# A two-layer mixer trunk on Trainium2: S5's direct products on four quarters of the array, retention's position factors moved to its values, S5's angles doubled in one run, LRU gates in small PSUM banks

## The chip, the core and the metric

The kernel runs on one core of one Trainium2 chip. TensorE multiplies, VectorE (DVE in the profile), ScalarE (ACT) and GpSimd (POOL) work on vectors, SyncE (SP) issues the transfers. The metric is device microseconds of one execution of the whole program; lower is better.

## What is computed

A trunk of two layers (`DEPTH = 2`) over 512 positions of width 1024 in float32. Each layer normalises its input, projects it, runs four token mixers of width 512 in parallel, gates and projects each, sums them under sigmoid gates and adds the projection of the sum:

```python
for l in range(DEPTH):
    u = rmsnorm(h, norm_gain[l])
    proj = u @ w_in[l]
    ...
    o_gla = gla_mix(...) * jax.nn.silu(gg)
    o_ret = retention_mix(rq, rk, rv, ...) * jax.nn.silu(rg)
    o_lru = rglru_mix(lx, ...) * jax.nn.silu(lg)
    y5 = jax.nn.gelu(s5_scan(su, ...))
    ...
    for bi, o in enumerate((o_gla, o_ret, o_lru, o_s5)):
        gate = jax.nn.sigmoid(u @ w_merge_gate[l, bi])
        merged = merged + gate * (o @ w_branch[l, bi])
    h = h + merged @ w_out[l]
return rmsnorm(h, final_norm_gain)
```

In retention, queries and keys are rotated by position, and factors that depend on the position in a chunk of 64 and on the head weight them: keys by `k_w` in the state, queries by `q_w` in front of the state, a decay between the two in the scores; each head's output is then normalised by its own mean and variance. RG-LRU needs per block two gates, sigmoids of a product with the block's convolved input, and a scan along time. S5 is a diagonal state-space model of 32 groups with 64 complex states, in blocks of 128 positions.

## The kernel before

**Products in three passes.** A float32 product is split into a high and a low part. Each weight tile of 128x1024 comes from memory into one of two raw buffers; ScalarE writes its high part (`hi`, L271), VectorE its low part (`lo`, L272), each into one of four buffers; then TensorE multiplies three times (L297 to L299 where the weight is the stationary operand, L391 to L393 in `proj_w` where the activations are). A raw buffer is free for the next transfer when the low part is written. All weights pass in one order of use.

**PSUM.** Three banks (`psm`, in the trace `pm`) serve the large products, five small ones (`pss`, `ps`) the rest. A bank comes back when the engine that evacuates it has read it.

**Order.** TensorE executes in the order in which the program is written. The order on the other engines is set by a scheduler that goes by its own estimates. Background work (attention, S5, LRU) is written as generators, which a tick after every few large matmuls advances by a step.

**The places of the change.** `s5_params` makes, for each layer, tables of sines and cosines by doubling: VectorE doubles an angle (`double`, L461 to L463) and copies the pair to `s5w` (L529, L530), and GpSimd (`grow`, L516 to L521) makes the next level of the table from it. It is written ahead of products that VectorE evacuates with L940 and L941 in the first layer, and ahead of the last merge (L1081) for the second. `s5_scan` has 8 groups per layer: `states` (L627) and `direct` (L637) multiply a group's input, `outputs` (L671) adds the state's part, ScalarE evacuates (L677); then comes a scan on VectorE. In `direct` the rows 64 to 127 of the array go with the columns 64 to 127, and the rows 0 to 63 with the columns 0 to 63. In `lru_block` a convolution (L1010) gives the block's input, split into xh and xl (L306); gate(0) and gate(1) (L1017) multiply it, ScalarE takes them through tanh, exp and square root (L1022 to L1037), VectorE and GpSimd combine them (L1030 to L1038), and VectorE scans (L1039, its result used by L1040). In retention `rotate` takes a tile of queries and keys: L1096 weights by the position factors (`gtab`) as it evacuates, L1103 (GpSimd) and L1105 multiply with sine and cosine, L1109 adds. The projection of the values follows, which ScalarE evacuates (L1121).

## Time and profile before

| what | value |
| --- | --- |
| median of 3 runs | 1243.51 us (1240.65 to 1243.98) |
| the profiled execution | 1242.54 us |
| its span in the trace | 1240.8 us |
| mean granted clock of TensorE, share of full speed | 0.991 |
| TensorE busy | 1205.1 us, 97% |
| VectorE busy | 816.8 us, 66% |
| ScalarE busy | 516.5 us, 42% |
| GpSimd busy | 508.0 us, 41% |
| moved by DMA | 127.89 MB, mean 103 GB/s |

Every time in the text is counted from the start of the span. Matmuls are pipelined, so the rows of two neighbours overlap; the distance of their starts is what one costs. "idle <- X" at a row's end is how long the engine had nothing to do before it, and what ended that.

### The profile page before, as it was taken

To read this page: it belongs to the slowest core of one execution; us is meant where nothing else is said; L and a number is where in the kernel's file an instruction comes from. 1 tells how busy PE (TensorE), PEld (TensorE's weight loads), DVE (VectorE), ACT (ScalarE), POOL (GpSimd) and SP (SyncE) were. 2 spreads that over 40 slices of the span, in tenths; PEclk is the share of its full clock that TensorE was granted. 3 is DMA by queue.
4 is the path that set the end of the run, shared out by engine and by line. 5 is a ranking of instruction groups with operands and counts; after the bars stand their busy time and mean duration, and the time that the engine had idled before them with its cause. 6 is when DMAs were issued, how large, how long until landed. Compare 5 with 4: busy or idle time off the path is not lost.

```text
span 1240.8 us, 17527 instructions
## 1 busy us (share of the span) xinstructions
PE 1205.1 (97%) x6649; PEld 990.5 (80%) x6649; DVE 816.8 (66%) x1479; ACT 516.5 (42%) x798; POOL 508.0 (41%) x547
## 2 busy tenths in 40 slices
PE   9989999989999999999999999999799999999997
PEld 7878768868888787888898887788688888888886
DVE  6686878686688678644355367776957986436433
ACT  5613475333434532432355235644244453324322
POOL 1473328988765159100201013397977551000001
PEclk9999999998999999999999999999899999999999
DMA  6334222322522442433343242233233233433322
GB/s 193 121 91 149 78 79 96 98 68 69 167 80 81 127 136 73 119 102 102 104 137 95 92 151 62 84 96 89 72 106 120 69 120 103 138 99 102 93 77 85
DMA packets 48758, 127.89 MB, mean 103 GB/s; under 512 B 6465, under 2 KB 19105, under 8 KB 48674
## 3 DMA queue, kind: packets, MB, share of 16 engines
q1 hardware_dynamic: 48098, 125.73, 32.6%
q8 instruction: 52, 0.85, 0.3%
q10 hardware_dynamic: 576, 1.05, 0.2%
q14 instruction: 32, 0.26, 0.1%
HBM read 118.37 MB, written 8.39 MB: 102 GB/s over the span
## 4 chain that ended last, share of the span: by engine, by line
PE 79%; DVE 8%; ACT 4%; POOL 4%; issue 2%; DMA 1%; SPq 0%; POOLq 0%; DVEq 0%; ACTq 0%
PE pm L297 20%; PE pm L298 19%; PE pm L299 19%; PE pm L391 4%; PE pm L392 4%; PE pm L393 4%; PE pm L370 3%; DVE lo L272 2%; PE ps L756 1%; PE ps L627 1%; PE ps L671 1%; PE ps L767 1%; PE ps L637 1%; PE ps L778 1%; ACT hi L271 1%
## 5 line engine op out<-in xcount | busy, mean ns | idle before, releaser
L272 DVE TENSOR_TENSOR lo<-raw,hi 128x1024 fp32r<-128x1024 f32 (+1 forms) x196 | 268.4, 1370 | 189.5 <-ACT hi L271 188.6
L297 PE MATMUL pm<-uh,hi 128*128 128x512 f32 x960 | 378.3, 394 | 7.3 <-ACT ac L1027 3.3
L299 PE MATMUL pm<-uh,lo 128*128 128x512 f32 x960 | 374.2, 390 | 0.0
L298 PE MATMUL pm<-ul,hi 128*128 128x512 f32 x960 | 373.9, 389 | 0.0
L271 ACT ACTIVATE hi<-raw 128x1024 fp32r<-128x1024 f32 (+1 forms) x196 | 207.4, 1060 | 399.0 <-PE pm L298 274.9
L297 PEld LDWEIGHTS pm<-uh,hi 128*128 128x128 f32 x960 | 180.2, 188 | 50.7 <-ACT ac L1027 5.0
L299 PEld LDWEIGHTS pm<-uh,lo 128*128 128x128 f32 x960 | 180.2, 188 | 38.1
L298 PEld LDWEIGHTS pm<-ul,hi 128*128 128x128 f32 x960 | 180.3, 188 | 36.3
L1226 POOL TENSOR_TENSOR ac<-c4a,S 128x512 f32<-128x512 f32 x2 | 2.6, 1295 | 248.6 <-DVE c4a L1224 248.6
L297 PE MATMUL pm<-oh,hi 128*128 128x512 f32 x256 | 101.0, 395 | 0.0
L299 PE MATMUL pm<-oh,lo 128*128 128x512 f32 x256 | 99.8, 390 | 0.0
L298 PE MATMUL pm<-ol,hi 128*128 128x512 f32 x256 | 99.7, 389 | 0.0
L391 PE MATMUL pm<-hi,uh 128*128 128x512 f32 x128 | 53.7, 419 | 12.8 <-DVE s L1096 12.8
L316 POOL TENSOR_TENSOR ty<-ty,c 128x4 f32<-128x4 f32 x16 | 17.6, 1103 | 102.9 <-DVE ty L314 102.6
L297 PEld LDWEIGHTS pm<-oh,hi 128*128 128x128 f32 x256 | 48.0, 188 | 11.2 <-issue 1.4
L299 PEld LDWEIGHTS pm<-oh,lo 128*128 128x128 f32 x256 | 48.0, 188 | 10.1
L298 PEld LDWEIGHTS pm<-ol,hi 128*128 128x128 f32 x256 | 48.1, 188 | 9.7
L392 PE MATMUL pm<-hi,ul 128*128 128x512 f32 x128 | 52.0, 406 | 0.0
L393 PE MATMUL pm<-lo,uh 128*128 128x512 f32 x128 | 51.9, 405 | 0.0
L1081 DVE SCALAR_TENSOR_TENSOR s<-s,pm 128x512 f32<-128x512 f32 x48 | 32.7, 682 | 14.8 <-PE pm L299 14.8
L391 PEld LDWEIGHTS pm<-hi,uh 128*128 128x128 f32 x128 | 25.4, 198 | 19.0 <-DVE s L1096 13.6
L647 DVE TENSOR_TENSOR r<-ps,cos 128x256 f32<-128x256 f32 x32 | 13.3, 422 | 39.5 <-ACT sw L646 39.5
(336 smaller groups left out, 2093.0 us busy)
## 6 DMA issues: line engine op xcount, KB each, us to landing
raw<-in_wch SPq DMA_DIRECT2D x192, 512.0 KB, 3.6
raw<-in_wgv SPq DMA_DIRECT2D x4, 544.0 KB, 4.7
uc<-in_x SPq DMA_DIRECT2D x4, 512.0 KB, 5.5
bc<-in_s5bc SPq DMA_DIRECT2D x16, 128.0 KB, 2.1
su_dram<-c4a SPq DMA_DIRECT2D x4, 512.0 KB, 2.8
uc<-su_dram SPq DMA_DIRECT2D x32, 64.0 KB, 2.6
y_dram<-uc SPq DMA_DIRECT2D x4, 512.0 KB, 4.8
v<-y_dram SPq DMA_DIRECT2D x32, 64.0 KB, 2.6
```

The source lines that it names most:

```text
L271: act.activation(hi, raw, AF.Copy)
L272: dve.tensor_tensor(lo, raw, hi.bitcast(F32), SUB)
L297: pe.matmul(ps, lh, rh, start=i == 0, stop=False)
L298: pe.matmul(ps, lh, rl, start=False, stop=False)
L299: pe.matmul(ps, ll, rh, start=False, stop=i == n - 1)
L316: pool.tensor_tensor(r, ms, neghalf[:, :n], ALU.pow)
L370: pe.matmul(ps[:, j], a[:, k, ts], ws[kh][b][:, k % 4], start=k == i == 0, stop=k == KD - 1 and i == 2)
L391: pe.matmul(ps[tt], xh(k, ts), wh, start=k == 0, stop=False)
L392: pe.matmul(ps[tt], xl(k, ts), wh, start=False, stop=False)
L393: pe.matmul(ps[tt], xh(k, ts), wl, start=False, stop=k == KD - 1)
L647: dve.tensor_tensor(r1[:, gg::2], pst[gg], cos[:, gg::2], MUL)
L1081: dve.scalar_tensor_tensor(t, t, 1.0, ps, op0=ADD, op1=MUL)
```

## The change

Four edits in one. `direct` sends each half of the rows to both halves of the columns in turn, so that its four products use all four quarters of the array; `outputs` and the way in which the result is read back follow that layout, and the evacuation becomes four pieces. In retention `gtab` no longer weights queries and keys: ScalarE copies the tile out of PSUM (L1100), VectorE and GpSimd rotate it (L1106, L1111, L1114), the values take the factor as they are evacuated, one piece per head (L1130), and the small constant in the variance is weighted to match. In `s5_params` all doublings are made in one run into a buffer with a place for each level. And `gate` takes a small bank.

```diff
-        wx = one("s5w", [P, 2, G])
+        wx = one("s5w", [P, 7, 2, G])
...
-        c4, sg4 = wx[:, 0], wx[:, 1]
-        double(sn, cs, sg4, c4)
-        double(sg4, c4, sn, cs)
-        dve.tensor_scalar(sg4, sn, sgn[:, 1:2], None, op0=MUL)
-        dve.tensor_copy(c4, cs)
+        double(sn, cs, ps_, pc_)
+        double(ps_, pc_, sn, cs)
+        dve.tensor_scalar(wx[:, 0, 0], sn, sgn[:, 1:2], None, op0=MUL)
+        dve.tensor_copy(wx[:, 0, 1], cs)
+        for i in range(6):
+            double(wx[:, i, 0], wx[:, i, 1], wx[:, i + 1, 0], wx[:, i + 1, 1])
...
-        for tab, nlev in ((bt, 4), (at, 3)):
+        for tab, lev0, nlev in ((bt, 0, 4), (at, 4, 3)):
...
-                grow(tab, 1 << lev, c4, sg4)
-                double(sg4, c4, sn, cs)
-                dve.tensor_copy(sg4, sn)
-                dve.tensor_copy(c4, cs)
+                grow(tab, 1 << lev, wx[:, lev0 + lev, 1], wx[:, lev0 + lev, 0])
...
-                    pe.matmul(st["bank"][gg][r, (2 + pr) * P:(3 + pr) * P], tz[r, pr], u2[r, pr],
-                              start=alone and pr == 0, stop=False, skip_group_check=True)
+                    o = 64 * (gg ^ pr)
+                    pe.matmul(st["bank"][gg][o:o + 64, (2 + pr) * P:(3 + pr) * P], tz[r, pr], u2[r, pr],
+                              start=alone, stop=False, skip_group_check=True)
...
-            for gg in range(2):
-                r = slice(64 * gg, 64 * gg + 64)
-                act.activation(u2[r], bank[gg][r, 2 * P:].rearrange("p (a b) -> p a b", a=2), AF.Copy)
+            for pr in range(2):
+                for half in range(2):
+                    r = slice(64 * half, 64 * half + 64)
+                    act.activation(u2[r, pr], bank[half ^ pr][r, (2 + pr) * P:(3 + pr) * P], AF.Copy)
...
             def gate(i):
-                g = psm()
+                g = pss()
...
-            xg = s2([P, 2, HEADS, 64])
-            dve.tensor_tensor(xg, ps.rearrange("p (a h d) -> p a h d", a=2, h=HEADS),
-                              gtab[:, :, :, None].to_broadcast([P, 2, HEADS, 64]), MUL)
+            xs = s2([P, 2, HEADS, 64])
+            act.activation(xs, ps.rearrange("p (a h d) -> p a h d", a=2, h=HEADS), AF.Copy)
...
-            dve.tensor_tensor(xv, xv, c[:, None].to_broadcast([P, 2 * HEADS, 2, 32]), MUL)
-            xf = xg.rearrange("p a h d -> p a (h d)")
...
-            for a, dst in ((1, krot), (0, qrot)):
-                dve.tensor_tensor(dst[:, tt], xf[:, a], mf[:, a], ADD)
+            for a, dst in dsts:
+                dve.tensor_tensor(dst[:, tt].rearrange("p (h d) -> p h d", h=HEADS), xs[:, a],
+                                  c[:, None].to_broadcast([P, HEADS, 64]), MUL)
+            for a, dst in dsts:
+                dve.tensor_tensor(dst[:, tt], dst[:, tt], mf[:, a], ADD)
...
-        proj_w(lambda tt, ps: act.activation(rv[:, tt], ps, AF.Copy), "in", u_hi, u_lo)
+        def evac_rv(tt, ps):
+            for h in range(HEADS):
+                hs = slice(h * DV, (h + 1) * DV)
+                act.activation(rv[:, tt, hs], ps[:, hs], AF.Copy, scale=gtab[:, 1, h:h + 1])
+        proj_w(evac_rv, "in", u_hi, u_lo)
...
-                r = rstd_of(mv[:, :, 1], HEADS, 1.0)
+                ms, r = tiny([P, HEADS]), tiny([P, HEADS])
+                dve.tensor_tensor(ms, mv[:, :, 1], gtab[:, 0], ADD)
+                pool.tensor_tensor(r, ms, neghalf, ALU.pow)
```

**Where instructions move.** The names below are those of the trace, with a running number behind them that differs between the two programs; line numbers are each program's own, so L1096 of before and L1100 of the changed kernel stand for the evacuation in `rotate`.

ScalarE in retention's projections of the first layer, before: `hi_2551`, `hi_2618` and `hi_2763` are the first three weights of the values, L681 and L685 belong to S5, L657 and L658 to its scan.

```order
L681 ACTIVATE s2_457_2590<-uc0_163_1037 128x512
L271 ACTIVATE hi_451_2551<-raw_450_2537 128x1024
L685 ACTIVATE s2_457_2590<-s2_457_2590 128x512
L271 ACTIVATE hi_461_2618<-raw_453_2555 128x1024
L657 ACTIVATE sw_471_2683<-gt_468_2652 64x512
L658 ACTIVATE sw_471_2683<-gt_468_2652 64x512
L271 ACTIVATE hi_487_2763<-raw_463_2622 128x1024
L271 ACTIVATE hi_492_2783<-raw_489_2767 128x1024
```

Between these rows ScalarE reads no bank of retention: VectorE empties all four tiles.

The same place of the changed kernel: `pm_469_2646` is the bank for which TensorE comes with the second tile of the values.

```order
L684 ACTIVATE s2_457_2577<-uc0_163_1020 128x512
L1100 ACTIVATE s2_464_2617<-pm_446_2504 128x512
L1100 ACTIVATE s2_466_2632<-pm_447_2511 128x512
L271 ACTIVATE hi_451_2536<-raw_450_2522 128x1024
L657 ACTIVATE sw_471_2672<-gt_468_2641 64x512
L658 ACTIVATE sw_471_2672<-gt_468_2641 64x512
L688 ACTIVATE s2_457_2577<-s2_457_2577 128x512
L271 ACTIVATE hi_461_2605<-raw_453_2540 128x1024
L271 ACTIVATE hi_487_2754<-raw_463_2609 128x1024
L1100 ACTIVATE s2_482_2729<-pm_469_2646 128x512
L1100 ACTIVATE s2_484_2744<-pm_470_2653 128x512
L271 ACTIVATE hi_492_2774<-raw_489_2758 128x1024
```

The evacuation of the third and fourth tile stands on ScalarE now, behind the split of the third weight (`hi_487`).

VectorE in the LRU blocks of the first layer, before: `ac2_281` is xl of block 2, made from `ac0_279`; L1036 and L1039 are the product ahead of the square root, and the scan, of block 1.

```order
L272 TENSOR_TENSOR lo_295_1772<-raw_292_1744,hi_294_1771 128x1024
L403 SCALAR_TENSOR_TENSOR of8_197_1267<-s2_289_1737,pm_275_1670 128x512
L1010 SCALAR_TENSOR_TENSOR ac0_279_1683<-pm_269_1627,pc_82_395,ac0_279_1683 128x509
L1036 SCALAR_TENSOR_TENSOR ac6_287_1716<-ac5_286_1715,ac6_287_1716 128x512
L272 TENSOR_TENSOR lo_313_1848<-raw_296_1775,hi_312_1847 128x1024
L306 TENSOR_TENSOR ac2_281_1685<-ac0_279_1683,ac1_280_1684 128x512
L1039 SCALAR_TENSOR_TENSOR ac4_246_1526<-ac6_287_1716,ac7_285_1714 128x512
L1040 SCALAR_TENSOR_TENSOR of8_197_1267<-ac4_246_1526,of8_197_1267 128x512
```

Here xl stands directly ahead of the scan.

The changed kernel, where L1039 is the product, L1042 the scan and L1043 the use of its result:

```order
L403 SCALAR_TENSOR_TENSOR of8_197_1250<-s2_289_1720,pm_275_1653 128x512
L1039 SCALAR_TENSOR_TENSOR ac6_287_1699<-ac5_286_1698,ac6_287_1699 128x512
L1013 SCALAR_TENSOR_TENSOR ac0_279_1666<-pm_269_1610,pc_82_395,ac0_279_1666 128x510
L272 TENSOR_TENSOR lo_313_1831<-raw_296_1758,hi_312_1830 128x1024
L1013 SCALAR_TENSOR_TENSOR ac0_279_1666<-pm_269_1610,pc_82_395,ac0_279_1666 128x509
L1042 SCALAR_TENSOR_TENSOR ac4_246_1509<-ac6_287_1699,ac7_285_1697 128x512
L1043 SCALAR_TENSOR_TENSOR of8_197_1250<-ac4_246_1509,of8_197_1250 128x512
L306 TENSOR_TENSOR ac2_281_1668<-ac0_279_1666,ac1_280_1667 128x512
```

The product ahead of the square root stands two convolution steps earlier, and xl behind the scan. The second layer has the same order.

VectorE at the parameters of the first layer, before: L461 to L463 double an angle, L530 and L529 copy it for GpSimd, and `pm_159` is the product that L940 and L941 evacuate last ahead of TensorE's next use.

```order
L461 SCALAR_TENSOR_TENSOR vt_133_726<-s5w_134_727 128x32
L462 SCALAR_TENSOR_TENSOR vt_133_726<-s5w_134_727 128x32
L463 TENSOR_SCALAR vt_133_726<-vt_133_726 128x32
L530 COPY s5w_134_727<-vt_133_726 128x32
L529 COPY s5w_134_727<-vt_133_726 128x32
L940 TENSOR_TENSOR e8_91_420<-pm_159_1007,e8_91_420 128x512
L941 TENSOR_TENSOR c4b_93_422<-pm_159_1007,c4b_93_422 128x512
```

The same evacuation in the changed kernel (now L943 and L944), with the last doubling at the head:

```order
L461 SCALAR_TENSOR_TENSOR vt_133_726<-s5w_134_727 128x32
L462 SCALAR_TENSOR_TENSOR s5w_134_727<-s5w_134_727 128x32
L463 TENSOR_SCALAR s5w_134_727<-vt_133_726 128x32
L272 TENSOR_TENSOR lo_157_985<-raw_154_955,hi_156_984 128x1024
L943 TENSOR_TENSOR e8_91_420<-pm_155_957,e8_91_420 128x512
L944 TENSOR_TENSOR c4b_93_422<-pm_155_957,c4b_93_422 128x512
L272 TENSOR_TENSOR lo_167_1024<-raw_158_988,hi_166_1023 128x1024
L943 TENSOR_TENSOR e8_91_420<-pm_159_990,e8_91_420 128x512
L944 TENSOR_TENSOR c4b_93_422<-pm_159_990,c4b_93_422 128x512
```

The doublings end ahead of both evacuations, and the copies are gone.

## Rows read from the trace of the kernel before

**Rows 1.** The page's busy times: us, share of the span, instructions.

```profile
PE 1205.1 (97%) x6649; PEld 990.5 (80%) x6649; DVE 816.8 (66%) x1479; ACT 516.5 (42%) x798; POOL 508.0 (41%) x547
```

**Rows 2.** TensorE's waits: line <- what ended them: us, times, longest.

```profile
PE pm L391 <- DVE s L1096: 12.8, 2, 6.4
PE ps L953 <- DVE c4b L941: 3.4, 1, 3.4
PE pm L297 <- ACT ac L1027: 3.3, 4, 1.5
PE pm L1017 <- ACT s L1022: 2.5, 4, 1.0
PE pm L297 <- DVE s L1081: 2.3, 1, 2.3
PE pm L297 <- ACT s L1022: 1.6, 2, 0.8
```

**Rows 3.** Timeline of TensorE behind retention's wait, layer 0: start, us, instruction.

```profile
279.56 0.80 PE L391 MATMUL pm<-hi,uh 128*128 128x512 f32 x1 [6.39 <-DVE s L1096]
...
285.59 0.39 PE L393 MATMUL pm<-lo,uh 128*128 128x512 f32 x1
285.82 0.39 PE L391 MATMUL pm<-hi,uh 128*128 128x512 f32 x1
```

**Rows 4.** Windows: length, busy us of each engine, granted clock, DMA share, GB/s.

```profile
276.00:280.00 4.00, 0.44 (x1) 0.44 (x2) 4.00 (x4) 0.90 (x1) 3.92 (x4) 0.50 0.29 102
88.00:93.00 5.00, 1.62 (x9) 1.14 (x8) 3.26 (x9) 0.00 (x0) 5.00 (x13) 1.00 0.36 105
```

**Rows 5.** Chain of waits in the window 255 to 282: start, us on the chain.

```profile
268.11 1.23 DVE lo L272
...
278.90 0.61 DVE s L1096
```

**Rows 6.** Timeline of ScalarE in retention's projections.

```profile
273.02 1.06 ACT L271 ACTIVATE hi<-raw 128x1024 fp32r<-128x1024 f32 x1 [3.43 <-DMA raw<-in_wch]
...
291.73 0.77 ACT L677 ACTIVATE uc<-ps 64x256 f32<-64x256 f32 x2 [2.63 <-PE ps L671]
...
294.38 0.36 ACT L613 ACTIVATE c<-ps,c 128x128 f32<-128x128 f32 x1
294.63 0.60 ACT L1121 ACTIVATE v<-pm 128x512 f32<-128x512 f32 x1
```

**Rows 7.** Groups by line and form: busy us, mean ns, idle before.

```profile
L1109 DVE TENSOR_TENSOR c4b<-s,s 128x256 f32<-128x256 f32 x8 | 7.8, 976 | 0.2
L1109 DVE TENSOR_TENSOR c4a<-s,s 128x256 f32<-128x256 f32 x8 | 4.8, 602 | 0.0
```

**Rows 8.** Timeline of TensorE: an S5 group, and a later matmul.

```profile
290.01 0.67 PE L627 MATMUL ps<-uc,vt 64*64 64x128 f32 x16
290.50 0.62 PE L637 MATMUL ps<-uc,c 64*64 64x128 f32 x8
291.04 0.66 PE L671 MATMUL ps<-r,c 128*64 128x128 f32 x8
...
295.19 0.40 PE L391 MATMUL pm<-hi,uh 128*128 128x512 f32 x1
```

**Rows 9.** Timeline of VectorE at the parameters, layer 0.

```profile
90.76 0.69 DVE L529 COPY s5w<-vt 128x32 f32<-128x32 f32 x1 [1.16 <-POOL cos L519]
```

**Rows 10.** Timeline at the LRU blocks, layer 0, first TensorE, then VectorE.

```profile
169.83 0.64 PE L1017 MATMUL pm<-ac,wbh 128*128 128x512 f32 x2
...
176.14 0.50 PE L297 MATMUL pm<-uh,hi 128*128 128x512 f32 x1 [1.47 <-ACT ac L1027]
...
167.50 0.68 DVE L1036 SCALAR_TENSOR_TENSOR ac<-ac,ac 128x512 f32<-128x512 f32 x1
...
169.23 0.68 DVE L306 TENSOR_TENSOR ac<-ac,ac 128x512 fp32r<-128x512 f32 x1
171.74 1.23 DVE L1039 TENSOR_TENSOR_SCAN ac<-ac,ac 128x512 f32<-128x512 f32 x1 [1.83 <-POOL ac L1038]
```

More of the change, by code (lines that the diff above doesn't have):

```diff
@@ L668, in outputs @@
             for pr in range(2):
-                for gg in range(2):
+                for half in range(2):
+                    gg, o = half ^ pr, 64 * half
                     g = 2 * pr + gg
-                    pe.matmul(bank[gg][64 * gg:64 * gg + 64, (2 + pr) * P:(3 + pr) * P],
+                    pe.matmul(bank[gg][o:o + 64, (2 + pr) * P:(3 + pr) * P],
                               caz[:, g, 1:5].rearrange("p a b -> p (a b)"), hp[:, g], start=False, stop=True,
@@ L674, in outputs @@
             yield
-            for gg in range(2):
-                r = slice(64 * gg, 64 * gg + 64)
-                act.activation(u2[r], bank[gg][r, 2 * P:].rearrange("p (a b) -> p a b", a=2), AF.Copy)
+            for pr in range(2):
+                for half in range(2):
+                    r = slice(64 * half, 64 * half + 64)
+                    act.activation(u2[r, pr], bank[half ^ pr][r, (2 + pr) * P:(3 + pr) * P], AF.Copy)
             if e % 2 == 1:
@@ L1094, in rotate @@
         def rotate(tt, ps):
-            xg = s2([P, 2, HEADS, 64])
-            dve.tensor_tensor(xg, ps.rearrange("p (a h d) -> p a h d", a=2, h=HEADS),
-                              gtab[:, :, :, None].to_broadcast([P, 2, HEADS, 64]), MUL)
+            xs = s2([P, 2, HEADS, 64])
+            act.activation(xs, ps.rearrange("p (a h d) -> p a h d", a=2, h=HEADS), AF.Copy)
+            xv = xs.rearrange("p a h (s d) -> p (a h) s d", s=2)
             m1 = s2([P, 2 * HEADS, 2, 32])
-            xv = xg.rearrange("p a h (s d) -> p (a h) s d", s=2)
-            c = rope[:, 0, tt].rearrange("p (s d) -> p s d", s=2)
+            c = rope[:, 0, tt]
             s = rope[:, 1, tt].rearrange("p (s d) -> p s d", s=2)
@@ L1104, in rotate @@
                                    s[:, hf][:, None, :].to_broadcast([P, 2 * HEADS, 32]), MUL)
-            dve.tensor_tensor(xv, xv, c[:, None].to_broadcast([P, 2 * HEADS, 2, 32]), MUL)
-            xf = xg.rearrange("p a h d -> p a (h d)")
             mf = m1.rearrange("p (a h) s d -> p a (h s d)", a=2)
-            for a, dst in ((1, krot), (0, qrot)):
-                dve.tensor_tensor(dst[:, tt], xf[:, a], mf[:, a], ADD)
+            dsts = (1, krot), (0, qrot)
+            for a, dst in dsts:
[3 more added lines that the diff above has]
+                dve.tensor_tensor(dst[:, tt], dst[:, tt], mf[:, a], ADD)
             def turn():
@@ L1174, in hybrid_kernel @@
             for j in range(8):
-                sp.dma_start(y5[16 * j:16 * j + 16, 2 * i:2 * i + 2], yv[j // 2, j % 2])
+                sp.dma_start(y5[16 * j:16 * j + 16, 2 * i:2 * i + 2], yv[j // 2, j % 2 ^ j // 2 % 2])
         y5n = y5.rearrange("p c t n -> p c n t")
@@ L1265, in shape_tables @@
     rope = rope.reshape(2, NT, P, 64).transpose(2, 0, 1, 3).astype(np.float32)
-    gt = np.stack([g[None, :] ** (i[:, None] % 64 + 1.0), DK ** -0.5 * g[None, :] ** (63.0 - i[:, None] % 64)], 1)
+    gt = np.stack([EPS * g[None, :] ** (-2.0 * (i[:, None] % 64 + 1.0)),
+                   DK ** -0.5 * g[None, :] ** (63.0 - i[:, None] % 64)], 1)
     perm = i[:, None] % 64 == np.arange(64)
```

## The prediction, written before the changed kernel ran

> **What bounds the kernel now.** I read the shares of busy time first: TensorE works for 97% of the span, the other engines for two thirds and less [rows 1]. So the time is TensorE's own work plus what it waits, and an edit counts only where it shortens one of the two. Next the list of TensorE's waits, summed by what ended them [rows 2]. The reader is to see that all six sums at its head belong to lines on which this change bears: 12.8 us on the first vector operation of retention's rotation (L1096), 3.4 and 2.3 us on L941 and L1081, which VectorE reaches late because small operations of layer parameters stand ahead, and 3.3 + 2.5 + 1.6 = 7.4 us on the LRU gates. Then the matmuls around the largest wait [rows 3] and the granted clock there [rows 4]: the clock stands at 0.50, its lower level, at the end of the wait, and 14 matmuls take 6.03 us from 279.56 to 285.59; from there on they start 0.23 us apart, at which 14 would take 3.2. So the wait costs 2.8 us more than its length. In the stretch with the wait of 3.38 us the clock stayed at 1.00 [rows 4]. One wait of retention is worth 6.4 + 2.8 = 9.2 us, and there is one in each layer.
>
> **Retention's rotation.** The chain of waits shows why VectorE is late [rows 5]: TensorE stops at 279.56 - 6.39 = 273.17 for a tile that L1096 reads only at 278.90, behind a queue that holds, among others, the split of a weight at 268.11. After the change ScalarE empties the tile (L1100), and VectorE's queue no longer decides. But the order on ScalarE puts this copy behind the split of the third weight of retention's values, which waits for its transfer; and the transfer needs the raw buffer that the split at 268.11 frees. That link is in the trace of before: the split ends at 269.34 [rows 5], and ScalarE's next one starts at 273.02, having waited for the transfer [rows 6]. So this transfer is late next. TensorE goes on at the end of VectorE's split plus 3.68 for the transfer, 1.06 for ScalarE's split, 0.60 for the copy (the price of L1121, ScalarE's too and of the same shape [rows 6]) and 0.1 to hand over: 5.45 us behind the split. Ahead of it VectorE had two L1096 (0.61 each [rows 5]), an L1105 of 128x512 and two L1109 of 128x256; now it has four multiplies and two additions of 128x256. Two inputs from SBUF at that size cost 0.60 or 0.98, the two means of L1109 [rows 7]. Counting L1105 as two such, six stand against four and 1.2 us: nothing at the lower price, 0.75 more at the higher. I take the lower, since the scan and S5's pieces around them stay. The split then ends at 269.3, TensorE goes on at 274.8 and has waited 1.6. It saves 4.8 and the half clock, 7.6 per layer, **15.3 in all**; 13.7 at the higher price, 18.4 with no wait left, nothing if the split came 4.8 later.
>
> Against it stands ScalarE's longer work at the next handover. Behind an S5 group it runs two evacuations (L677), six further copies and L1121, which ends at 295.23 [rows 6]; TensorE's matmul at 295.19 starts without a wait [rows 8], so there is no slack. Four evacuations of 64x128 replace two of 64x256 (0.77 together), and four of 128x128 with a scale replace L1121's 0.60. In the row of L613, of 128x128, the next operation starts 0.25 later. Four such last 1.0; at L677's price, 0.39 for one, 1.5. That is 0.2 to 0.8 and 0.4 to 0.9 more; I take 0.3 + 0.5, near L613: a new wait of 0.8 per layer, **1.6 lost** (1.2 to 3.4). Elsewhere these evacuations lie beside a matmul stream that runs on; with that cover gone each S5 group would add its 0.2 to 0.8. The scale of r (one small vector operation for another) and the order in which S5's result is read back leave the counts as they were and cost nothing.
>
> **S5's direct products.** In an S5 group L627 issues 16 records over all four quarters of the array from 290.01 to 290.50; L637 issues 8 of the same shape on two quarters and takes longer, 0.54 [rows 8]. On twice as many quarters it should take half, 0.27; some hundredths go to the change of line whatever the quarters, so I take 0.25 saved in each of 16 groups, **4.0 us**, between nothing and 0.295 x 16 = 4.7 (L627's rate). TensorE issues them back to back, so all of it is on the path.
> The Trainium skill, TensorEngine Tiling (Array Packing), Restrictions and Gotchas, says that two row tiles cannot access one PSUM bank at a time. This speaks against products that now cross to the other half of the columns: wherever they shared a bank they would run in turn, nothing would be gained, and the sum would be 4.0 higher. Here each half of the rows keeps a bank of its own, as it does in L627, whose row shows the overlap.
>
> **Doubled angles.** Each copy L529 or L530 waits for GpSimd's table, and all behind it on VectorE waits along: the copy at 90.76 waited for L519 and holds up L940 and L941 behind it, and TensorE waits for L941 [rows 2, 9]. In the new order the doublings stand ahead of this and need nothing from GpSimd; L944 follows its matmuls behind one weight split. In layer 1 it is L1081 that stands behind such copies. Both waits go: 3.4 + 2.3 = **5.7 us**, or nothing if GpSimd still reached VectorE, through a buffer that both use; in the new order no row does.
>
> **LRU gates.** With gates in the small banks the 7.4 us go. But VectorE's order changes too: block 2's xl (L306), which stood ahead of block 1's scan, now stands behind the scan and the product after it. The scan waits for GpSimd, that for ScalarE's square root, that for L1036. Before, L1036 started at 167.50 and the scan at 171.74, 4.24 later, while xl was done at 169.91, just in time for the gate at 169.83 [rows 10]. In the new order two operations less stand ahead of L1036 (1.3 us at its own price, 0.68), and one weight split more (1.23 [rows 5]) stands in the block before, on the same chain but partly under ScalarE's work. I take 0.6 earlier, and 0.8 for the first of the waits that go: 166.1. The scan is then at 170.3 and takes 1.23; product and xl take 0.65 each: xl is done at 172.8. TensorE comes 2.0 earlier, at 167.8 (per layer half of the 7.4, less the 1.47 at the merge [rows 10] and about 0.25 at block 2's second gate), and waits. From xl to the merge are 17 matmuls of 0.23, so the merge starts at 176.7, where it started at 176.14: 0.5 lost per layer. **The 7.4 us go and 8.4 come back, 1.0 lost.** Bounds: all 7.4 kept if xl were in time; 2 x 2.8 more lost if the clock fell in the new wait. The matmul on xh cuts that wait in two, and 3.38 us left the clock alone, so I don't expect it.
>
> **Sum.** -15.3 + 1.6 - 4.0 - 5.7 + 1.0 = -22.4, from the profiled execution's 1242.54 (span 1240.8 and 1.7 around it): 1220.1. The runs' median is 1.0 above that execution, so I write 1220.5.
>
> **Rivals.** (1) LRU's gain stays: the chain to xl is shorter than I add up. 8.4 better: 1212. For it speaks that an order gives no times; against it that three engines stand in line between L1036 and xl. (2) LRU's wait lets the clock fall in both layers: 5.6 more, 1226. (3) Retention's transfer comes late: the split ends at 271.5 or behind it, 3.8 us or more of the wait remain and the half clock with it, so 5 us or less are saved there: 1230 to 1236. For it speaks the dearer L1109. (4) The direct products don't overlap across column halves: 1224. (5) Not faster: vector operations stretch beside GpSimd, and more of them read SBUF than before. L1096 read PSUM and took 0.61; its successors read SBUF twice. Each microsecond by which the split at 269.3 comes later costs one per layer. At 274.1 the old wait is back with its 2.8; the other terms (4.0 + 5.7 - 1.6 - 1.0 = 7.1, 3.6 per layer) are used up at 277.7. From there the kernel is slower. Six operations would have to take 2.0 each, twice the dearer mean, so this is unlikely.
> The Trainium skill, SBUF — State Buffer, Who interferes with whom, states that a vector instruction with two SBUF inputs contends with GpSimd's reads, and one with a single SBUF input doesn't. Here the rows agree (0.60 and 0.98 for half the size of L1096's 0.61), and by that rule it is this change that brings the contention into the multiply.
>
> **Chances.** My forecast 0.42, with a range of its own of 1216 to 1225; (1) 0.16; (2) 0.10; (3) 0.16; (4) 0.08; (5) 0.08, half of it within 0.3% (3.7 us, about what the runs can tell from no change), half slower. So faster 0.92, same 0.04, slower 0.04. The range 1209 to 1232 leaves out (5) and the upper part of (3).
>
> **What the new profile would show.** L637's stretch in a group near 0.3 instead of 0.54. In retention's projections no wait on VectorE, but one of 1 to 2 us on ScalarE's L1100 at a clock of 1.00, and some tenths on ScalarE's L1130. No wait on L944 and L1084. In LRU none for a gate's bank, but 4 to 5 us in each layer on xl (L306). I am wrong if that wait is missing (then 1212), if the one on L1100 is over 3 us with the clock at 0.50 behind it, or if a place that has cover now begins to wait, S5's longer evacuation above all.

## The result and the profile after

The changed kernel takes 1228.64 us, median of 4 runs (1227.32 to 1229.39), against 1243.74 of the kernel before in 4 (1240.65 to 1245.23): a ratio of 0.9881, 95% interval 0.9865 to 0.9896. It is 15 us faster. The profiled execution took 1228.44 us, its span is 1226.7: 14.1 less than before, where the sum of the prediction had said 22.4. The direction held, and 1228.64 lies within the wide range of 1209 to 1232, but outside the forecast's own range of 1216 to 1225.

First the page's busy times.

```profile
PE 1200.6 (98%) x6649; PEld 988.4 (81%) x6649; DVE 816.7 (67%) x1445; ACT 530.2 (43%) x862; POOL 513.9 (42%) x547
```

TensorE bounds the kernel as before [rows 1]. It works 4.5 us less and is idle 9.6 us less (the rest of the 14.1). TensorE's waits, line <- what ended them, us, times, longest:

```profile
PE pm L391 <- ACT s L1100: 7.5, 2, 3.9
PE ps L1020 <- DVE ac L306: 4.6, 2, 2.3
PE pm L297 <- DVE of L403: 1.7, 2, 0.9
PE ps L1020 <- ACT ac L305: 1.6, 2, 0.8
```

Against [rows 2]: the two waits behind the angles (L941, L1081) are gone. The 7.4 us at the LRU gates' banks are gone, and 4.6 + 1.7 + 1.6 = 7.9 stand in their place. Retention's 12.8 became 7.5, on ScalarE's copy instead of VectorE. There the prediction's own sign of being wrong is met: over 3 us on L1100 in both layers (3.87 and 3.59), with the clock at its lower level behind.

The sum by place is got by following the same matmul through both traces, ahead of a place and behind it. Starts in us:

| place | ahead: before, after | behind: before, after | change |
| --- | --- | --- | --- |
| parameters, layer 0 | 86.19, 86.21 | 97.79, 94.24 | -3.6 |
| LRU, layer 0 | 141.19, 137.64 | 182.39, 179.77 | +0.9 |
| retention, layer 0 | 266.44, 263.37 | 289.00, 282.31 | -3.6 |
| merge with the second layer's parameters | 477.34, 469.79 | 498.09, 487.92 | -2.6 |
| LRU, layer 1 | 752.28, 742.50 | 793.91, 785.08 | +1.0 |
| retention, layer 1 | 873.43, 864.15 | 900.54, 887.33 | -3.9 |

So angles -6.2 (predicted -5.7), LRU +1.9 (+1.0), retention -7.5 (-15.3 + 1.6 = -13.7). S5's direct products give -3.4 (-4.0), by the groups below. The rest, +1.1, is spread over the span. Of the 8.3 us that are missing, retention is short of 6.2.

**Retention after.** TensorE's timeline at the first layer's wait (start, us, instruction), and a window with the granted clock (the column ahead of the last two):

```profile
273.97 0.50 PE L391 MATMUL pm<-hi,uh 128*128 128x512 f32 x1 [3.87 <-ACT s L1100]
...
275.16 0.63 PE L392 MATMUL pm<-hi,ul 128*128 128x512 f32 x1
275.59 0.63 PE L393 MATMUL pm<-lo,uh 128*128 128x512 f32 x1
...
278.41 0.40 PE L391 MATMUL pm<-hi,uh 128*128 128x512 f32 x1
```

```profile
276.00:280.00 4.00, 4.00 (x14) 3.19 (x13) 4.00 (x5) 1.07 (x1) 4.00 (x5) 0.72 0.61 204
```

TensorE stopped at 270.10, waited 3.87 us, and then its clock stood at the lower level (1.2 GHz) for part of the next stretch: matmuls start 0.43 apart there instead of 0.23. The 12 starts from 273.97 to 278.41 take 4.44 us; 0.23 each would be 2.76, so the stretch costs 1.7. Before, that was 2.8 behind a wait of 6.39 [rows 3]. Per layer 6.39 + 2.8 became 3.87 + 1.7 (3.59 + 1.7 in the second): the -3.6 and -3.9 of the table.

Why the copy is late is seen on ScalarE and VectorE. ScalarE's timeline:

```profile
272.38 1.06 ACT L271 ACTIVATE hi<-raw 128x1024 fp32r<-128x1024 f32 x1 [2.81 <-DMA raw<-in_wch]
273.34 1.07 ACT L1100 ACTIVATE s<-pm 128x512 f32<-128x512 f32 x2
```

VectorE's timeline ahead of the split whose end lets that transfer start:

```profile
257.59 1.32 DVE L618 SCALAR_TENSOR_TENSOR c<-c,sd,c 128x64 f32<-128x64 f32 x2
...
259.92 1.22 DVE L649 TENSOR_TENSOR r<-r,sw 128x512 f32<-128x512 f32 x1
261.06 0.96 DVE L1111 TENSOR_TENSOR c4b<-s,c 128x256 f32<-128x256 f32 x1
261.94 0.87 DVE L1111 TENSOR_TENSOR c4a<-s,c 128x256 f32<-128x256 f32 x1
262.73 3.85 DVE L653 TENSOR_TENSOR_SCAN gt<-s5f,r 128x128 f32<-128x128 f32 x4
266.51 0.45 DVE L1114 TENSOR_TENSOR c4b<-c4b,s 128x256 f32<-128x256 f32 x1
266.88 0.51 DVE L1114 TENSOR_TENSOR c4a<-c4a,s 128x256 f32<-128x256 f32 x1
267.32 1.30 DVE L272 TENSOR_TENSOR lo<-raw,hi 128x1024 fp32r<-128x1024 f32 x1
```

The link that the prediction named holds: the split ends at 268.62, the transfer lands, ScalarE splits and copies, TensorE goes on at 273.97, 5.35 us behind the split (predicted 5.45). But the split's end came only 0.7 earlier than before (269.34, [rows 5]), while TensorE and all work ahead came 3.1 earlier. From the first L614 of the group (256.26) to the split's end VectorE needs 12.36 us; before, from the same operation (there L615), 9.85. Rows of that stretch before:

```profile
259.49 0.64 DVE L615 SCALAR_TENSOR_TENSOR c<-ps,c,c 128x96 f32<-128x96 f32 x2 [0.24 <-ACT c L613]
...
260.80 0.85 DVE L649 TENSOR_TENSOR r<-r,sw 128x512 f32<-128x512 f32 x1
261.57 0.82 DVE L619 SCALAR_TENSOR_TENSOR c<-c,sd,c 128x64 f32<-128x64 f32 x2
...
262.92 2.67 DVE L653 TENSOR_TENSOR_SCAN gt<-s5f,r 128x128 f32<-128x128 f32 x4
```

L619 there is L618 of the changed kernel.

**LRU after.** VectorE's, then TensorE's timeline in the first layer, against [rows 10]:

```profile
165.43 1.23 DVE L1042 TENSOR_TENSOR_SCAN ac<-ac,ac 128x512 f32<-128x512 f32 x1 [0.99 <-POOL ac L1041]
...
167.30 0.68 DVE L306 TENSOR_TENSOR ac<-ac,ac 128x512 fp32r<-128x512 f32 x1
```

```profile
168.03 0.50 PE L1020 MATMUL ps<-ac,wbh 128*128 128x512 f32 x1 [2.31 <-DVE ac L306]
...
171.67 0.63 PE L1020 MATMUL ps<-ac,wbl 128*128 128x512 f32 x1
```

The product L1039 starts at 161.28 and the scan 4.15 behind it (predicted 4.2), and xl comes last, as foreseen. Counted with TensorE's own shift of 3.6, L1039 stands at 164.8 where I had 166.1. TensorE's wait is cut into pieces of 0.85, 0.80 and 2.31 (3.96 per layer, predicted 4.2). The records of 0.63 behind the third piece, where the clock stands at its lower level, are the prediction's second rival, to which it gave 0.10.

**S5's direct products after**, TensorE's timeline of a group, against [rows 8]:

```profile
283.32 0.67 PE L626 MATMUL ps<-uc,vt 64*64 64x128 f32 x16
283.81 0.40 PE L637 MATMUL ps<-uc,c 64*64 64x128 f32 x8
284.14 0.66 PE L673 MATMUL ps<-r,c 128*64 128x128 f32 x8
```

From the first L637 to the first L673 it is 0.33 us, where it was 0.54: 0.21 in each of 16 groups, 3.4.

### The profile page after: what moved, and what is told of

Read it like the earlier page. It is cut to its first block, busy times and chain, and to the rows that moved or that the text cites. A ratio compares the mean times of both kernels' runs of the same rounds, so it can differ in the third digit from the quotient of the medians.

```text
span 1226.7 us, 17548 instructions
## 1 busy us (share of the span) xinstructions
PE 1200.6 (98%) x6649; PEld 988.4 (81%) x6649; DVE 816.7 (67%) x1445; ACT 530.2 (43%) x862; POOL 513.9 (42%) x547
## 4 chain that ended last, share of the span: by engine, by line
PE 89%; DVE 5%; ACT 2%; issue 2%; POOL 1%; DMA 1%; POOLq 0%; ACTq 0%; DVEq 0%
PE pm L297 23%; PE pm L299 22%; PE pm L298 22%; PE pm L391 4%; PE pm L392 4%; PE pm L393 4%; PE pm L370 3%; PE ps L759 1%; DMA raw<-in_wch 1%; DVE lo L272 1%; PE ps L626 1%; PE ps L673 1%; PE ps L1020 1%; DVE gt L653 1%; PE ps L781 1%
## 5 line engine op out<-in xcount | busy, mean ns | idle before, releaser
L272 DVE TENSOR_TENSOR lo<-raw,hi 128x1024 fp32r<-128x1024 f32 (+1 forms) x196 | 273.0, 1394 | 199.2 <-ACT hi L271 190.5
L316 POOL TENSOR_TENSOR ty<-ty,c 128x4 f32<-128x4 f32 x8 | 8.8, 1100 | 93.6 <-DVE ty L314 93.6
L1084 DVE SCALAR_TENSOR_TENSOR s<-s,pm 128x512 f32<-128x512 f32 x48 | 32.8, 683 | 14.4 <-PE pm L299 9.6
L661 POOL TENSOR_TENSOR sw<-sw,sin 128x512 f32<-128x512 f32 x16 | 26.1, 1631 | 27.9 <-ACT sw L658 27.9
L1075 ACT ACTIVATE s<-pm 128x512 f32<-128x512 f32 x64 | 37.2, 581 | 0.1
```

The lines of the kernel that those rows point to most:

```text
L272: dve.tensor_tensor(lo, raw, hi.bitcast(F32), SUB)
L661: pool.tensor_tensor(sw, sw, sin, MUL)
L1075: act.activation(ts[-1], gps, AF.Tanh, scale=0.5)
L1084: dve.scalar_tensor_tensor(t, t, 1.0, ps, op0=ADD, op1=MUL)
```

## The experiments

My theory of the missing time: in retention VectorE's queue ahead of the split stretches beside GpSimd, and in LRU the wait on xl brings the clock down. The rivals: the order on ScalarE (copies behind a split) costs the time, or the parts work against each other. Line numbers are each program's own. The kernel before, measured beside each group, had medians of 1243.89 (first four kernels), 1242.58 (next four) and 1242.63 (last four). The changed kernel's 1228.64 stands beside 1243.74, so a difference to it in us is good to about 1 us, and the ratios say what is resolved. Where a place is named, one traced execution of each kernel is compared.

### One part at a time

Each kernel is the one before with one of the four edits of the change's diff.

S5's direct products alone:

```diff
+                    o = 64 * (gg ^ pr)
+                    pe.matmul(st["bank"][gg][o:o + 64, (2 + pr) * P:(3 + pr) * P], tz[r, pr], u2[r, pr],
```

> The kernel before with the direct products (and the four-piece evacuation and the read-back that go with them) alone. Theory A, by the trace of the changed kernel: each of 16 groups shortens from 0.54 to 0.33 us, all of it on TensorE's path, so 3.4 us faster (0.27%), L637's stretch 0.33. Rival B: what TensorE saves here it waits for later, on VectorE in retention, since that queue does not start earlier: 1 us or nothing.

Measured: 1242.43, ratio 0.9991 (0.9982 to 0.9999). The first line of TensorE's waits:

```profile
PE pm L391 <- DVE s L1099: 14.4, 2, 7.2
```

The products themselves give their 0.21 per group, but retention's wait grows from 12.8 to 14.4, and the clock stands low once more, near 490, which cost 1.4 in the traced execution. TensorE came earlier at a place where it waits for VectorE, so 1.6 of the 3.4 turned into waiting there. That the edit keeps its whole 3.4 with the retention edit beside it alone was not run.

Retention alone:

```diff
-            dve.tensor_tensor(xg, ps.rearrange("p (a h d) -> p a h d", a=2, h=HEADS),
-                              gtab[:, :, :, None].to_broadcast([P, 2, HEADS, 64]), MUL)
+            act.activation(xs, ps.rearrange("p (a h d) -> p a h d", a=2, h=HEADS), AF.Copy)
...
+                act.activation(rv[:, tt, hs], ps[:, hs], AF.Copy, scale=gtab[:, 1, h:h + 1])
```

> The kernel before with retention's edit alone (copy on ScalarE, rotation, values scaled). Theory A: the wait falls from 6.4 to about 3.9 us per layer, as in the changed kernel, and the clock still falls behind it, but for 3.4 us instead of 10.2: 6 to 8 us faster. Rival B, the prediction's sum: the wait falls to 1.6 us with the clock at 1.00, 13 to 15 us faster.

Measured: 1238.13, ratio 0.996 (0.9946 to 0.9974). The first line of TensorE's waits:

```profile
PE pm L391 <- ACT s L1096: 8.0, 2, 4.0
```

4.0 us of wait per layer without any other edit: the shortfall lies in the retention edit itself. Here TensorE's own shift is only 0.2 us, so the split can be held against the 269.3 of the prediction directly. VectorE's timeline:

```profile
271.21 1.23 DVE L272 TENSOR_TENSOR lo<-raw,hi 128x1024 fp32r<-128x1024 f32 x1 [1.02 <-ACT hi L271]
```

It ends at 272.44, 3.1 late. In this kernel 1.02 of that is a wait for ScalarE's high part, most of the rest VectorE's longer work; in the changed kernel VectorE doesn't stop in the stretch.

Angles alone:

```diff
+        for i in range(6):
+            double(wx[:, i, 0], wx[:, i, 1], wx[:, i + 1, 0], wx[:, i + 1, 1])
...
-                double(sg4, c4, sn, cs)
-                dve.tensor_copy(sg4, sn)
-                dve.tensor_copy(c4, cs)
```

> The kernel before with the angles doubled in one run, alone. Theory A: both waits (3.4 and 2.3 us) go, nothing comes back, 5.7 us faster (0.46%). Rival B: TensorE comes 3.4 us earlier to LRU and retention and waits there for the slower engines, so 3 us or less are left.

Measured: 1235.12, ratio 0.9933 (0.992 to 0.9945), 8.8 below the kernel before. Both waits on L941 and L1081 are gone, retention's stays at 12.8. Followed from matmul to matmul, 3.6 come at the first layer's parameters and 2.6 at the merge: 6.2, as in the whole change; another 0.3 comes at the second layer's retention, where the clock rose sooner. The profiled executions differ by 6.5 (1236.05 for 1242.54). The medians show more, 6.8 to 10.0 by the interval: the profiled execution of the kernel before lies 1.35 below its median here, this one 0.9 above its own. What the other executions did otherwise no trace shows.

Gates in small banks alone:

```diff
-                g = psm()
+                g = pss()
```

> The kernel before with the LRU gates in small banks, alone. Theory A: the waits for a bank (3.7 us per layer) go, the waits on xh, xl and L403 come (4.0 us per layer), and the clock falls behind them for 3.4 us: no faster, 0 to 4 us slower. Rival B: alone the gates keep VectorE's old order of xl and scan and gain the 7.4 us; it is the other parts that spoil it.

Measured: 1246.24, ratio 1.0021 (1.001 to 1.0032). The largest of the waits at LRU, and the window behind it with the granted clock:

```profile
PE ps L1017 <- DVE ac L306: 4.6, 2, 2.3
```

```profile
170.00:180.00 10.00, 7.20 (x18) 5.49 (x19) 5.91 (x9) 5.21 (x8) 0.66 (x1) 0.66 0.18 54
```

The edit alone makes the kernel slower: with 1.7 and 1.6 behind L403 and L305 it waits as much as before, and the clock is low at three more places, here (0.66), in the second layer's LRU near 788, and between 93 and 98. The last lies ahead of the gates, behind a wait of 3.5 us that the edit does not touch and that left the clock alone in the three other kernels that have it (3.4 to 3.5 us); it is 1.7 of the 3.4 us by which this traced execution is longer. The four parts add up to -1.5 - 5.8 - 8.8 + 2.3 = -13.8, near the whole's 15.

### What is late in LRU, and in retention

xl ahead of the scan: the changed kernel, with block 1's scan issued behind the newest xl.

```diff
-            split(xh, xl, xc)
+            newest.append(split(xh, xl, xc))
...
-            dve.tensor_tensor_scan(xc, rl, gl, 0.0, MUL, SUB)
+            with tc.issue_after(newest[-1].ins):
+                dve.tensor_tensor_scan(xc, rl, gl, 0.0, MUL, SUB)
```

> The changed kernel with one order constraint: the LRU scan is issued behind the newest xl, so VectorE makes block 2's xl ahead of block 1's scan again. Theory A (the order of xl and scan costs the gates their gain): TensorE's wait on xl falls from 2.3 to 0.5 us per layer, and the clock stays at 1.00 there: 1228.6 less 3.6 and 3.2, 1222. Rival B (xh on ScalarE and the bank of L403 would hold TensorE just as long): 1227 to 1229.

Measured: 1221.06, ratio 0.9827 (0.9812 to 0.9842), 7.6 below the changed kernel (6.7 by the ratios). The wait on xl, and a window with the granted clock:

```profile
PE ps L1022 <- DVE ac L306: 0.6, 2, 0.3
```

```profile
160.00:172.00 12.00, 10.07 (x42) 7.46 (x41) 10.34 (x17) 9.74 (x13) 2.53 (x2) 1.00 0.36 100
```

The wait on xl falls by 4.0, and the clock stays at 1.00, where the changed kernel has 0.87 in the same window. By place, LRU gives 3.6 and 3.7: 2.0 is the wait, 1.6 and 1.7 the clock. So the place of one instruction of 0.68 us decided whether the gates' edit gains.

Copies ahead of the split, on ScalarE: the high part of the third weight issued behind retention's copies.

```diff
-        act.activation(hi, raw, AF.Copy)
+        with tc.issue_after(copied[-1].ins) if copied else nullcontext():
+            act.activation(hi, raw, AF.Copy)
```

> The changed kernel with ScalarE's copies of the third and fourth tile of retention's queries and keys (L1100) ahead of the split of the third weight, so they no longer stand behind its transfer. Theory A (VectorE's queue as a whole is late): the wait on the copy goes, but TensorE then waits some 3 us per layer for the low part of the second weight, which VectorE finishes at 274.6: 1226 to 1228. Rival B, the link that the prediction named is the whole cause: 7.5 us of waits and the fall of the clock go, 1218.

Measured: 1232.9, ratio 0.9924 (0.9906 to 0.9942), 4 slower than the changed kernel. The first line of TensorE's waits:

```profile
PE pm L395 <- DVE lo L274: 8.4, 4, 2.4
```

TensorE no longer waits for the copy, but in each layer for the low parts of the second and the third weight (2.4 and 1.8), and it is slower than either theory had. The copy is only the last to arrive; the weights are late.

Low parts ahead of S5's pieces, on VectorE: in retention's projections S5's scan and the product behind it are issued behind two low parts.

```diff
+        lows.append(dve.tensor_tensor(lo, raw, hi.bitcast(F32), SUB))
...
+            with behind(-2):
+                for g in range(4):
...
+            with behind(-1):
+                dve.tensor_tensor(gt, gt, cos, MUL)
```

> The changed kernel with VectorE's split of the first weight of retention's values ahead of S5's scan in that stretch, and the split of the second ahead of the product behind the scan. The transfer can start 3 us earlier, nothing changes on ScalarE but its order around S5's exchange. Theory A: the wait on L1100 falls from 3.7 to under 2 us per layer and the clock stays at 1.00: 1221. Rival B: the delayed scan is what the next handover needs, and the wait moves there: 1227 or more.

Measured: 1226.27, ratio 0.9871 (0.9855 to 0.9888), not resolved from the changed kernel's 0.9881. The waits of TensorE in retention:

```profile
PE pm L395 <- ACT s L1106: 4.0, 2, 2.0
PE pm L303 <- DVE lo L276: 2.3, 2, 1.1
PE pm L301 <- ACT v L1138: 1.9, 2, 1.0
```

With the split earlier, the wait on the copy is 2.0 per layer and the clock stays at 1.00 in retention. By the places of the table retention gives 3.4 and 3.2 more than in the changed kernel, but 2.7 and 3.0 are lost directly behind: on the next low parts, and on the values' evacuation (L1138), which here becomes a wait such as the prediction had put into the changed kernel. Another 1.6 of the traced execution has nothing to do with this repair. In the first layer's LRU TensorE waits in the same three pieces as in the changed kernel (0.86, 0.79 and 2.31), and here the clock stays up:

```profile
160.00:172.00 12.00, 8.04 (x33) 5.77 (x32) 9.81 (x15) 7.72 (x10) 2.50 (x2) 1.00 0.32 89
```

Both together:

```diff
+        with tc.issue_after(copied[-1].ins) if copied else nullcontext():
+            act.activation(hi, raw, AF.Copy)
...
+            with behind(-2):
+                for g in range(4):
```

> The changed kernel with both: the copies ahead of the third weight's split on ScalarE, and the two low parts ahead of S5's scan and product on VectorE. Theory A: neither the copy nor a low part is late by more than 0.7 us, the clock stays at 1.00: 1228.6 less 6 to 7.5 and 3.2, 1218 to 1219.5. Rival B: the wait goes on to the third weight's low part, which now stands behind four multiplies: 1223 or more.

Measured: 1231.2, ratio 0.991 (0.9895 to 0.9925). The first line of TensorE's waits:

```profile
PE pm L399 <- DVE lo L278: 9.1, 2, 4.6
```

The wait is whole again, on the third weight's low part. I had expected the two repairs to add up; the rival, that the wait moves on to this weight, was right. Rearranging the two queues does not buy back what VectorE's time costs.

### What stretched VectorE

GpSimd quiet: its products in the rotation and in S5's preparation are replaced by constants written to the same places.

```diff
-                pool.tensor_tensor(m1[:, :, hf], xv[:, :, 1 - hf],
-                                   s[:, hf][:, None, :].to_broadcast([P, 2 * HEADS, 32]), MUL)
+                pool.memset(m1[:, :, hf], 0.0)
...
-            pool.tensor_tensor(x1, ce(CP), cc(0), MUL)
-            pool.tensor_tensor(x2, ce(CQ), cc(1), MUL)
+            pool.memset(x1, 0.5)
+            pool.memset(x2, 0.5)
```

> The changed kernel with GpSimd's six products that read two operands in rotate and in S5's preparation (L1106, L560, L561, L568, L569) left out: GpSimd writes a constant of the same size instead, so the output is another. VectorE's work is the same. Theory A (vector operations with two inputs in SBUF stretch beside GpSimd's reads): the scan falls from 3.85 to about 1.9 us, L1111 from 0.75 to 0.42 in the mean, the split that ended at 268.62 ends 3 us earlier, and retention's wait of 3.7 us per layer falls under 1: some 9 to 11 us faster than the changed kernel's 1228.6. Rival B (VectorE simply has that much to do): the durations stay, the waits too, 1227 or more.

Measured: 1218.42, ratio 0.9809 (0.9795 to 0.9824), 10.2 below the changed kernel (8.9 by the ratios). TensorE's wait on the copy, then VectorE's timeline at the place shown above:

```profile
PE pm L391 <- ACT s L1100: 1.2, 2, 0.6
```

```profile
257.42 0.69 DVE L618 SCALAR_TENSOR_TENSOR c<-c,sd,c 128x64 f32<-128x64 f32 x2
...
259.72 0.41 DVE L1110 TENSOR_TENSOR c4b<-s,c 128x256 f32<-128x256 f32 x1
260.06 0.41 DVE L1110 TENSOR_TENSOR c4a<-s,c 128x256 f32<-128x256 f32 x1
260.39 2.48 DVE L653 TENSOR_TENSOR_SCAN gt<-s5f,r 128x128 f32<-128x128 f32 x4
262.80 0.40 DVE L1113 TENSOR_TENSOR c4b<-c4b,s 128x256 f32<-128x256 f32 x1
...
263.78 0.41 DVE L1113 TENSOR_TENSOR c4a<-c4a,s 128x256 f32<-128x256 f32 x1
264.13 1.21 DVE L272 TENSOR_TENSOR lo<-raw,hi 128x1024 fp32r<-128x1024 f32 x1
```

From L614 at 256.08 to the split's end at 265.34 it is 9.26 us instead of 12.36, with the same operations in the same order up to the scan and then four additions ahead of the split (L1113) where the changed kernel has two: more work in less time. L618 takes 0.69 instead of 1.32, the scan 2.48 instead of 3.85 (I had expected 1.9), a multiply 0.41 instead of up to 0.96. L614 and L647, which read one of their inputs from PSUM, last as long as in the changed kernel (0.32, 0.56 and 0.42). The wait falls to 0.6 and the clock stays up. By place, retention gains 8.5 us per layer against the kernel before, 17.0 in all, where the prediction had 15.3; GpSimd is quieter here than in the kernel before, so this is more than the change could have given. So the mechanism and its price were right, but for VectorE's pace.

S5's scan left out of the one group per layer that lies beside the rotation (ScalarE copies instead):

```diff
+            if rot:
+                act.activation(gt, r1, AF.Copy)
+            for g in range(0 if rot else 4):
```

> The changed kernel with S5's scan left out in the one group per layer that runs beside retention's queries and keys: ScalarE copies there instead, so the output is another, and VectorE has 3.85 us less to do ahead of the weight split. Theory A (retention's wait is the length of VectorE's queue): the wait on L1100 falls from 3.7 to under 1 us per layer, no wait takes its place, the clock stays at 1.00: 1218 to 1220. Rival B (the transfer and ScalarE's order set it): the wait stays above 2.5 us, 1226 or more.

Measured: 1225.63, ratio 0.9867 (0.9852 to 0.9881), not resolved from the changed kernel's 0.9881; the profiled run is the slowest of the four, at 1228.08. The gain that I expected is not there. VectorE's timeline ahead of the split, and a new wait of TensorE:

```profile
263.80 0.85 DVE L1117 TENSOR_TENSOR c4b<-c4b,s 128x256 f32<-128x256 f32 x1
...
264.58 1.52 DVE L1117 TENSOR_TENSOR c4a<-c4a,s 128x256 f32<-128x256 f32 x1
266.02 1.23 DVE L663 TENSOR_TENSOR gt<-gt,cos 128x512 f32<-128x512 f32 x1
267.18 1.76 DVE L273 TENSOR_TENSOR lo<-raw,hi 128x1024 fp32r<-128x1024 f32 x1
```

```profile
PE pm L298 <- ACT v L1135: 1.8, 2, 1.0
```

3.85 us of scan went, but the product L663 moved up into its place (1.23), the two additions took 2.37 instead of 0.96, and the split 1.76 instead of 1.30: 3.85 - 1.23 - 1.41 - 0.46 = 0.75. The wait is 3.1 per layer, and the clock stays up behind it. By place retention gains 2.3 and 2.2 against the changed kernel, and it is lost again: 1.1 and 1.3 at the LRU, where behind the same waits the clock is low for longer, the rest on the values' evacuation (L1135). The additions now lie beside GpSimd's four operations from 262.76 to 267.85 (L561, L562, L689, L1109): what is no longer stretched in the scan is stretched in its neighbours.

Gates back in large banks, all else as in the changed kernel:

```diff
-                g = pss()
+                g = psm()
```

> The changed kernel with the LRU gates back in the large banks. Theory A (gates in small banks with the order that follows are a loss): the old waits of 3.7 us per layer return in place of 4.0, and the clock stays at 1.00 there: 1224 to 1226, faster than the changed kernel. Rival B (the other parts need the free banks): 1228 to 1231.

Measured: 1227.6, ratio 0.9874 (0.9858 to 0.9891), within the interval of the changed kernel and between the two theories. LRU's waits are 7.3 again and its clock stays up, which gives 0.9 in the first layer against the changed kernel; retention's low stretch is longer (13 starts from 272.89 to 278.60, 5.71 us) and takes 0.9 back. The gates' edit as it stands is worth nothing that these runs resolve; with xl ahead of the scan it is worth some 6.5 (1221.06).

Both repairs, xl ahead of the scan and low parts ahead of S5's pieces:

```diff
+            with tc.issue_after(newest[-1].ins):
+                dve.tensor_tensor_scan(xc, rl, gl, 0.0, MUL, SUB)
...
+            with behind(-2):
+                for g in range(4):
```

> The changed kernel with both order constraints that gained: the scan of the LRU behind the newest xl, and VectorE's low parts ahead of S5's scan in retention. Theory A: the gains add, 1221.1 less some 1.2: 1219 to 1220.5, faster than before, than the changed kernel and than either alone. Rival B: with the LRU 4 us shorter, retention's waits grow, and it is no better than 1221.

Measured: 1219.55, ratio 0.9814 (0.9799 to 0.9828). The first line of TensorE's waits:

```profile
PE pm L395 <- ACT s L1109: 3.6, 2, 1.9
```

23 us below the kernel before, 9 below the changed kernel, with nothing left out. Its lead over the repair of xl alone, 1.5, is not resolved by these runs. In retention the clock stays up in the first layer, behind a wait of 1.70, and falls in the second, behind one of 1.94; the window there:

```profile
869.50:873.00 3.50, 3.50 (x10) 2.72 (x9) 3.50 (x3) 1.06 (x1) 3.50 (x3) 0.51 0.26 104
```

By place that is 7.4 us against the kernel before in the first layer and 5.5 in the second.

## Why the prediction came out as it did

**Angles**: right in mechanism and size (both waits gone).

**Direct products**: right; 0.21 per group instead of 0.25. The stretch of 0.33 is what the four quarters give, and no bank stood in the way, as L627's row [rows 8] had said.

**Retention**: the mechanism was right, one term mis-sized. The step that failed is "the split then ends at 269.3", with VectorE's work ahead of it priced at "nothing at the lower price, 0.75 more at the higher". It ended at 268.62, but with TensorE 3.1 earlier, which is 271.7 on the prediction's scale (272.4 with the retention edit alone): the third rival's condition (271.5 or behind), which had 0.16. Its 5 us or less became 7.5, since the low clock behind the wait cost less than the 2.8 it reckoned with. What made the split late is the fifth rival's mechanism, at another place than it looked. The six new operations did cost what the four old ones cost: 0.41 + 0.83 + 0.96 + 0.87 + 0.45 + 0.51 = 4.03, against 0.68 + 0.68 + 1.59 + 0.42 + 0.52 = 3.89 of the kernel before. But I held the neighbours constant ("since the scan and S5's pieces around them stay"), and it is these that grew: the scan from 2.67 to 3.85, L618 from 0.82 to 1.32, L649 from 0.85 to 1.22, and an L647 of 0.42 fell into the stretch. With the 0.14 above that is 2.6, the 2.5 by which the stretch grew. The quiet GpSimd takes all of it back, so it is contention with GpSimd, shown. The Trainium skill, SBUF — State Buffer, Who interferes with whom, states the rule that the prediction cited in its fifth rival. The runs agree: 1.32 against 0.69 and 3.85 against 2.48 us with two SBUF inputs, no change at L614 and L647. The prediction applied it to the new operations alone and not to what already stands there. That the neighbours grew because they now lie beside other GpSimd work fits the kernel without the scan, but no run puts them back to show it.

Nor was the half clock "gone": 1.7 per layer stayed. That is 3.4 of the missing 6.2, the longer waits (7.5 instead of 3.2) another 4.3; the evacuation, priced at 1.6 and free, gives 1.6 back. Without that the time would have been about 1230, so part of the nearness to the forecast is luck.

**Longer evacuations**: wrong. "There is no slack" read the matmul at 295.19 [rows 8] as the one that needs the bank that L1121 empties [rows 6]. That matmul starts before L1121 ends at 295.23, so it can't need its bank: by the program the three banks go in turn, and the one that L1121 empties is needed six matmuls later, at 296.57. L1130 appears in no wait of the changed kernel. In some kernels whose VectorE order differs it does (1.0 per layer with the low parts ahead, 0.9 without the scan), in the quiet one not.

**LRU**: the wait on xl came as foreseen, 7.9 for 8.4. The second rival, the clock that falls behind it, was given 0.10 and happened, at 1.6 to 1.7 per layer instead of 2.8. The reason against it, that 3.38 us in one piece had left the clock alone, carried nothing: 0.85, 0.80 and 2.31 in pieces brought it down here, and in 12 of the 14 layers of traced kernels that wait in these pieces. Waits (+0.5) and clock (+3.3) would make +3.8, and the table has +1.9. In part this is because five stops per layer became three, and a stop costs more than its idle time (the next start follows after 0.34 instead of 0.23); the rest stays open.

**Parts**: the sum was made as if terms were independent. The direct products alone gave 1.5 of 3.4, the gates alone lost 2.3 (in part to a low clock ahead of them) where beside the others they are even: what one edit saves ahead of a wait, the wait takes, and the clock behind it follows its own course.

## What to carry to other kernels

Price a vector operation by the whole stretch of its queue up to the instruction that matters, not by itself: with GpSimd running beside it, its neighbours can grow although the work itself costs the same. When a buffer edit moves an instruction behind a scan, look for the one engine that needs it next, and pin the order; here that one line was worth about 7 us. And where a wait stands at the end of a chain through a transfer, gains ahead of it are lost in it until the start of that transfer is moved.

## What was not expected of the hardware

The granted clock did not follow the length of a wait. It stayed at 1.00 behind single waits of 3.38 us [rows 4] and of 3.1 in the kernel without the scan, and fell behind 3.87 and 3.59 of the changed kernel, but also behind one of 1.94 in the kernel with both repairs. Nor did the same waits always do the same: the three pieces at the LRU, of at most 2.31, brought it down in both layers of the changed kernel and left it at 1.00 in one layer each of two others. A low stretch of the changed kernel cost 1.6 to 1.7 us, one of the kernel before 2.8. What decides it these runs leave open; it also means that a microsecond or two between two traced executions can be the clock and not the edit.

And four scans of 128x128 took between 1.36 and 3.86 us within the changed kernel, with nothing changed in the instruction, only in what ran beside it. In the first group it is 2.23 in the changed kernel, and 1.36 in the quiet one, where GpSimd does nothing from 207.76 to 211.28 beside the scan at 208.47.
